# Interleaving two tensors through SBUF: eight tiles with rows of 31.5 KiB and a ninth small one, in place of eight tiles with rows of 32 KiB

## The chip, the cores and the metric

The kernel runs on one core of a Trainium2 chip. The metric is the device time of one execution in microseconds (us), the median of several runs. The profile comes from one execution that the hardware profiler recorded; its times count from the first instruction.

## What is computed

Two inputs x and y of shape 32 x 256 x 1024 in fp32 (33.5 MB each) are woven into one output of 32 x 256 x 2048: even places of the last dimension from x, odd places from y.

```python
result = np.zeros((batch, seq, dim * 2), dtype=np.float32)
result[..., 0::2] = x
result[..., 1::2] = y
```

Seen flat, each of the three tensors is one contiguous run, and element i of x and of y go to elements 2i and 2i+1 of the output. So the work can be cut at any element, without regard to the shape.

## The kernel before

The flat inputs are cut into n = 8 tiles of 128 partitions by W = 8192 columns, 4 MiB each: a partition's row is 32 KiB, contiguous in memory, and the next partition's row follows directly on it (`rows`, L18 to L20). The output tile that belongs to it has rows of 64 KiB; it is made and stored in two pieces, of 4096 input columns each, so a store moves 128 rows of 32 KiB that stand 64 KiB apart.

On chip there are two buffers each for x, y and output pieces (`xt`, `yt`, `ot`, L23 to L25), every one of 32 KiB per partition. Tile k uses `xt` and `yt` number k % 2; its piece h uses `ot` number h.

Three engines carry the order of the work, each in program order:

- SP (SyncE) issues the loads: x of tile k, then y of tile k (L42 to L50). From tile 2 on, the load of x waits until the last x copy of tile k - 2 is done, and the load of y until its last y copy is (semaphore `woven`, which every copy counts up by one, four per tile).
- VectorE (DVE) weaves (L52 to L65). For each piece it copies the columns of x into the even places of `ot[h]` (L62) and the columns of y into the odd ones (L65). Ahead of the x copy it waits for the load of x and for the store that used `ot[h]` before (`osem[h]`); ahead of the first y copy of a tile for the load of y.
- ACT (ScalarE) issues the stores (L67 to L73), each when both copies of its piece are done.

The first tile's x is loaded in two halves, one issued on SP (L38) and one on ACT (L41). ACT also issues a tiny transfer of 16 rows of 512 B straight from x into the output (L40), whose bytes the first store later overwrites. The first transfer on each of the two engines is moved ahead into the program's opening block (L91 to L110), so that it starts before the engines meet.

At the end ACT waits for the last store from `ot[0]` and clears the semaphores (L75 to L78); SP waits for the last store from `ot[1]` and counts its semaphore down (L79). SP's transfers run on the DMA queue called q1 in the profile, ACT's on q10; both feed the same 16 DMA engines.

Of the kernel before, what the change touches and what calls it, by code (L numbers as in the profile page):

```python
# [3 lines left out]


def _interleave(nc, x, y, out):
    P = 128
    W = 8192
    H = W // 2  # L10

    total = 1
    for s in x.shape:
        total *= s
    n = total // (P * W)
    assert n * P * W == total

    def rows(ap, names, k):  # L18
        flat = ap.rearrange("b s d -> (b s d)")
        return flat[k * names : (k + 1) * names].rearrange("(p w) -> p w", p=P)  # L20

    fp32 = mybir.dt.float32
    xt = [nc.alloc_sbuf_tensor(f"xt{b}", [P, W], fp32).ap() for b in (0, 1)]  # L23
    yt = [nc.alloc_sbuf_tensor(f"yt{b}", [P, W], fp32).ap() for b in (0, 1)]
    ot = [nc.alloc_sbuf_tensor(f"ot{b}", [P, W], fp32).ap() for b in (0, 1)]  # L25

    xsem = [nc.alloc_semaphore(f"xsem{b}") for b in (0, 1)]
    hsem = nc.alloc_semaphore("hsem")
    tsem = nc.alloc_semaphore("tsem")
    ysem = [nc.alloc_semaphore(f"ysem{b}") for b in (0, 1)]  # L30
    woven = nc.alloc_semaphore("woven")
    osem = [nc.alloc_semaphore(f"osem{b}") for b in (0, 1)]

    xs = [rows(x, P * W, k) for k in range(n)]
    ys = [rows(y, P * W, k) for k in range(n)]
    os_ = [rows(out, 2 * P * W, k) for k in range(n)]

    nc.sync.dma_start(out=xt[0][:, :H], in_=xs[0][:, :H]).then_inc(xsem[0], 16)  # L38
    few = (slice(0, P, P // 16), slice(0, 128))
    nc.scalar.dma_start(out=os_[0][few], in_=xs[0][few]).then_inc(tsem, 16)  # L40
    nc.scalar.dma_start(out=xt[0][:, H:], in_=xs[0][:, H:]).then_inc(hsem, 16)  # L41
    for k in range(n):  # L42
        b = k % 2
        if k >= 2:
            nc.sync.wait_ge(woven, 4 * (k - 2) + 3)
        if k:
            nc.sync.dma_start(out=xt[b], in_=xs[k]).then_inc(xsem[b], 16)
        if k >= 2:
            nc.sync.wait_ge(woven, 4 * (k - 2) + 4)
        nc.sync.dma_start(out=yt[b], in_=ys[k]).then_inc(ysem[b], 16)  # L50

    for k in range(n):  # L52
        b = k % 2
        for h in (0, 1):
            c = slice(h * H, (h + 1) * H)
            if h == 0:
                nc.vector.wait_ge(xsem[b], 16 * (k // 2 + 1))
            elif k == 0:
                nc.vector.wait_ge(hsem, 16)
            if k:  # L60
                nc.vector.wait_ge(osem[h], 16 * k)
            nc.vector.tensor_copy(out=ot[h][:, 0::2], in_=xt[b][:, c]).then_inc(woven, 1)  # L62
            if h == 0:
                nc.vector.wait_ge(ysem[b], 16 * (k // 2 + 1))
            nc.vector.tensor_copy(out=ot[h][:, 1::2], in_=yt[b][:, c]).then_inc(woven, 1)  # L65

    nc.scalar.wait_ge(tsem, 16)  # L67
    for k in range(n):
        for h in (0, 1):
            nc.scalar.wait_ge(woven, 4 * k + 2 * h + 2)  # L70
            nc.scalar.dma_start(
                out=os_[k][:, h * W : (h + 1) * W], in_=ot[h]
            ).then_inc(osem[h], 16)  # L73

    nc.scalar.wait_ge(osem[0], 16 * n)  # L75
    used = sorted(s.num for s in [*xsem, hsem, tsem, *ysem, woven, osem[0]])
    assert used == list(range(used[0], used[-1] + 1)), used
    nc.scalar.sem_clear(range(used[0], used[-1] + 1))  # L78
    nc.sync.nop(nofuse=True).wait_op(osem[1], 16 * n, "sem-ge").then_inc(  # L79
        osem[1], -16 * n  # L80
    )


def kernel(tc, x, y, out):
    nc = tc.nc
    tc.close()
    tc.compile()

    _interleave(nc, x, y, out)

    blocks = nc.main_func.blocks  # L91
    for engine in (mybir.EngineType.SP, mybir.EngineType.Activation):
        opening = blocks[0].instructions
        at, moved = next(
            (b, i)
            for b in blocks[1:]
            for i in b.instructions
            if i.engine == engine and i.opcode == "DMACopy"
        )
        assert not (moved.sync_info and moved.sync_info.on_wait)  # L100
        body = at.instructions
        body.remove(moved)
        gate = next(
            n
            for n, i in enumerate(opening)
            if i.engine == engine and i.opcode == "Drain"
        )
        opening.insert(gate, moved)
        at.instructions = body
        blocks[0].instructions = opening  # L110


# [1 line left out]
_INS = ['x', 'y']  # L114
_OUTS = [((32, 256, 2048), 'float32')]


# [23 lines left out]
```

## Time and profile before

| | us |
|---|---|
| median of 3 runs (lowest, highest) | 314.57 (314.43, 314.57) |
| span of the profiled execution | 313.0 |
| median of the runs less that span | 1.57 |
| DVE busy | 72.6 |
| idle of DVE ahead of the x copies, in all | 180.2 |
| idle of DVE ahead of the y copies, in all | 45.4 |
| one copy of 128 x 4096, x and y | 2.295 and 2.292 |
| store of 4 MiB, issue to landing, median | 29.1 |
| load of x, of y, 4 MiB, issue to landing, median | 43.7 and 60.9 |
| data moved | 134.23 MB |
| mean rate over the span | 429 GB/s |

The profiled execution has no time of its own beside its span; what a run takes around the span is seen in the third row. How to read the page: its DMA line gives the busy share of the 16 DMA engines in 40 equal slices, in tenths; the queue lines give packets, megabytes and the time of the packets as a share of 16 engines' span. The table by stage gives, for a stretch of time, the busy time of each engine with the number of instructions in brackets, the granted TensorE clock (not used here), the DMA share and the rate. A line of groups or of the order of time names the source line, the engine, the operation, the tile written and the tile read.

### The profile page before, as it was taken

What the parts mean: (1) busy time and instruction counts of PE and PEld (TensorE: products, weight loads), DVE (VectorE), ACT (ScalarE), POOL (GpSimd) and SP (SyncE); (2) the same over time, 40 slices, a digit from 0 to 9 for tenths busy, and PEclk for the clock granted to TensorE, in tenths of its full rate; (3) what the DMA queues carried; (4) which work ended last, traced back from release to release, by engine and by line L of the source; (5) the groups of instructions that cost most, each with busy time, mean ns of one, the idle gap of its engine ahead of it and who ended that gap; (6) DMA issues with size and microseconds to landing.
All of it is one profiled execution on the core that took longest, in us unless ns stands there. A gap on an engine that the chain in (4) does not pass through costs nothing.

```text
span 313.0 us, 115 instructions
## 1 busy us (share of the span) xinstructions
DVE 72.6 (23%) x32; POOL 0.2 (0%) x4
## 2 busy tenths in 40 slices
DVE  0216002231022410325003250031501305013510
POOL 0000000000000000000000000000000000000000
DMA  8999999999999999999999999999999999999998
GB/s 336 435 435 402 465 406 452 419 448 423 435 435 419 452 402 469 402 469 402 465 406 452 419 448 423 435 435 419 452 402 469 402 469 402 465 406 452 419 448 356
DMA packets 4784, 134.23 MB, mean 429 GB/s; under 512 B 544, under 2 KB 560, under 8 KB 560
## 3 DMA queue, kind: packets, MB, share of 16 engines
q10 hardware_dynamic: 2480, 69.22, 51.2%
q1 hardware_dynamic: 2304, 65.01, 48.5%
HBM read 67.12 MB, written 67.12 MB: 429 GB/s over the span
## 4 chain that ended last, share of the span: by engine, by line
DMA 82%; DVE 12%; issue 0%
DMA out_dram<-ot 76%; DVE ot L65 6%; DMA yt<-in_y_dram 6%; DVE ot L62 6%
## 5 line engine op out<-in xcount | busy, mean ns | idle before, releaser
L62 DVE COPY ot<-xt 128x4096 f32<-128x4096 f32 x16 | 36.7, 2295 | 180.2 <-DMA out_dram<-ot 171.5
L65 DVE COPY ot<-yt 128x4096 f32<-128x4096 f32 x16 | 36.7, 2292 | 45.4 <-DMA yt<-in_y_dram 45.4
L125 POOL MEMSET const-bfloat16-1.0<- 128x1 bf16 x1 | 0.1, 101 | 0.0
L125 POOL MEMSET const-uint8-127<- 128x1 uint8 x1 | 0.1, 101 | 0.0
L125 POOL MEMSET const-float32-1.0<- 128x1 f32 x1 | 0.1, 99 | 0.0
L125 POOL MEMSET const-float32-0.0<- 128x1 f32 x1 | 0.1, 98 | 0.2 <-issue 0.2
## 6 DMA issues: line engine op xcount, KB each, us to landing
out_dram<-ot ACTq DMA_DIRECT2D x16, 4096.0 KB, 29.1
yt<-in_y_dram SPq DMA_DIRECT2D x8, 4096.0 KB, 60.9
xt<-in_x_dram SPq DMA_DIRECT2D x7, 4096.0 KB, 43.7
xt<-in_x_dram SPq DMA_DIRECT2D x1, 2048.0 KB, 8.7
xt<-in_x_dram ACTq DMA_DIRECT2D x1, 2048.0 KB, 17.5
out_dram<-in_x_dram ACTq DMA_DIRECT2D x1, 8.0 KB, 6.1
```

Of the source, the lines that this page charges most:

```text
L62: nc.vector.tensor_copy(out=ot[h][:, 0::2], in_=xt[b][:, c]).then_inc(woven, 1)
L65: nc.vector.tensor_copy(out=ot[h][:, 1::2], in_=yt[b][:, c]).then_inc(woven, 1)
L125: nc = _bacc.Bacc("TRN2", target_bir_lowering=False, num_devices=1)
```

## The change

W becomes 8064, so a row is 31.5 KiB. The columns per partition in all, 65,536, are eight times 8064 and 1024 left over, which make a ninth tile (rows of 4 KiB in x and in y, of 8 KiB in the output). The first eight tiles are woven and stored in two pieces of 4032 columns, the ninth in one piece of 1024, so there are 17 pieces in place of 16. Piece i uses `ot[i % 2]`. The waits are the same ones, counted by pieces; the ninth tile's loads wait for the last copies of the seventh (number 6), like every other load for the tile two before. The last piece is now in `ot[0]`, so the two closing waits change places and the semaphores are allocated in the order that keeps the cleared ones together. The buffers shrink with W.

```diff
-    W = 8192
-    H = W // 2
+    W = 8064
...
-    n = total // (P * W)
-    assert n * P * W == total
+    assert total % P == 0
+    cols = total // P
+    widths = [W] * (cols // W)
+    if cols % W:
+        widths.append(cols % W)
+    n = len(widths)
...
+    fx, fy, fo = flat(x), flat(y), flat(out)
+    at = [P * sum(widths[:k]) for k in range(n)]
+
+    def rows(ap, k, scale=1):
+        a, w = scale * at[k], scale * widths[k]
+        return ap[a : a + P * w].rearrange("(p w) -> p w", p=P)
...
+    pieces = []
+    for k, w in enumerate(widths):
+        step = w // 2 if w > W // 2 else w
+        pieces += [(k, c, c + step) for c in range(0, w, step)]
+    last = {}
+    for i, (k, _, _) in enumerate(pieces):
+        last[k] = i
+    m = len(pieces)
+    end = (m - 1) % 2
...
     for k in range(n):
         b = k % 2
         if k >= 2:
-            nc.sync.wait_ge(woven, 4 * (k - 2) + 3)
+            nc.sync.wait_ge(woven, 2 * last[k - 2] + 1)
         if k:
-            nc.sync.dma_start(out=xt[b], in_=xs[k]).then_inc(xsem[b], 16)
+            load(xt[b], fx, k, xsem[b])
         if k >= 2:
-            nc.sync.wait_ge(woven, 4 * (k - 2) + 4)
-        nc.sync.dma_start(out=yt[b], in_=ys[k]).then_inc(ysem[b], 16)
+            nc.sync.wait_ge(woven, 2 * last[k - 2] + 2)
+        load(yt[b], fy, k, ysem[b])
...
+    for i, (k, a, e) in enumerate(pieces):
+        b = k % 2
+        if a == 0:
+            nc.vector.wait_ge(xsem[b], 16 * (k // 2 + 1))
+        elif k == 0:
+            nc.vector.wait_ge(hsem, 16)
+        if i >= 2:
+            nc.vector.wait_ge(osem[i % 2], 16 * (i // 2))
+        o = ot[i % 2][:, : 2 * (e - a)]
+        nc.vector.tensor_copy(out=o[:, 0::2], in_=xt[b][:, a:e]).then_inc(woven, 1)
+        if a == 0:
+            nc.vector.wait_ge(ysem[b], 16 * (k // 2 + 1))
+        nc.vector.tensor_copy(out=o[:, 1::2], in_=yt[b][:, a:e]).then_inc(woven, 1)
...
+    for i, (k, a, e) in enumerate(pieces):
+        nc.scalar.wait_ge(woven, 2 * i + 2)
+        nc.scalar.dma_start(
+            out=rows(fo, k, 2)[:, 2 * a : 2 * e], in_=ot[i % 2][:, : 2 * (e - a)]
+        ).then_inc(osem[i % 2], 16)
...
-    nc.scalar.wait_ge(osem[0], 16 * n)
+    nc.scalar.wait_ge(osem[1 - end], 16 * (m // 2))
...
+    turns = (m + 1) // 2
+    nc.sync.nop(nofuse=True).wait_op(osem[end], 16 * turns, "sem-ge").then_inc(
+        osem[end], -16 * turns
+    )
```

`load(tile, ap, k, sem)` issues on SP the load of the first `widths[k]` columns of a tile.

## The prediction

> **What bounds the kernel now.** I read the page first, then the busy table by stage, then the packet view of single stretches, the waits and the order of time at the end. The page:
>
> ```profile
> span 313.0 us, 115 instructions
> ...
> DMA  8999999999999999999999999999999999999998
> ...
> DMA packets 4784, 134.23 MB, mean 429 GB/s; under 512 B 544, under 2 KB 560, under 8 KB 560
> ...
> q10 hardware_dynamic: 2480, 69.22, 51.2%
> q1 hardware_dynamic: 2304, 65.01, 48.5%
> ```
>
> The 16 DMA engines are busy from end to end, and the two queues' shares add to 99.7%. The chain of waits says the same in another way: 82% of it is DMA, nearly all stores. VectorE (DVE) is busy for 72.6 of 313.0 us, and what it idles for is the stores:
>
> ```profile
> DVE ot L62 <- DMA out_dram<-ot: 171.5, 14, 19.3
> DVE ot L65 <- DMA yt<-in_y_dram: 45.4, 8, 11.0
> ```
>
> That alone doesn't yet say that the stores wait for nobody. The table by stage does (stretch, its length, DVE and POOL busy, clock, DMA share, GB/s):
>
> ```profile
> 0.00:2.00 2.00, 0.00 (x0) 0.20 (x4) 1.00 0.62 123
> 2.00:24.00 22.00, 4.27 (x2) 0.00 (x0) 1.00 1.03 441
> 24.00:30.00 6.00, 4.73 (x3) 0.00 (x0) 1.00 0.92 355
> ...
> 106.04:144.75 38.71, 9.08 (x4) 0.00 (x0) 1.00 1.00 433
> 144.75:183.49 38.74, 9.09 (x5) 0.00 (x0) 1.00 1.00 433
> ...
> 287.60:303.30 15.70, 6.79 (x3) 0.00 (x0) 1.00 1.01 434
> ```
>
> From 30 us on the share is 1.00 and the rate 433 GB/s, whether loads and stores mix (106 to 183) or stores run alone (287 to 303). So no wait of any engine reaches the end: the sum of the DMA engines' work does. Only two places run below that rate, the first 2 us and the stretch from 24 to 30, where the first store joins.
>
> **The price of a row.** The page's packets can be counted out. Each row of a transfer is one packet, and each transfer adds 16 small ones, its completion counts. Per engine: 16 half rows of the first x tile (16 KiB), 7 x 8 rows of x, 8 x 8 of y and 16 x 8 of stores at 32 KiB, one row of 512 B, 34 completions: 299, and 16 x 299 = 4784. One tile in the steady stretch is 32 rows and 4 completions per engine in 38.72 us (the mean of the two stretches above). The trace's packet records give a completion 9 ns, so a row costs (38,720 - 36) / 32 = 1,209 ns, or 37.8 ns per KiB. The records themselves show a 32 KiB row lasting 1,213 ns, a 16 KiB row 611 ns and a 512 B row 27 ns.
>
> **The change part by part.**
>
> 1. *Rows of 31.5 KiB.* The same 264 rows per engine, each 1/64 shorter: 256 whole-row equivalents lose 18.9 ns each, 4.84 us. The bytes taken off are those of the ninth tile: per engine 16 rows of 4 KiB (x and y) and 8 of 8 KiB (store) are 128 KiB, at 37.8 ns per KiB 4.84 us again. Bytes are conserved, so these two cancel, and what counts is what a row costs beside its bytes.
> 2. *24 more rows per engine.* Their fixed cost is not in the trace for these sizes, so from both sides. Below: in one stretch of 1,209 ns (7.25 to 8.46 us) the records show two 16 KiB rows per engine, as much time as one 32 KiB row: fixed cost 0. Above: the 512 B row has 27 ns, of which 18.9 are its bytes: 8 ns, so 24 x 8 = 0.20 us. Between them, 611 less half of 1,213 is 4.5 ns; the new rows lie nearer in size to that one, so 24 x 4.5 = 0.11 us.
> 3. *Three more transfers.* 3 x 9 ns of completions, 0.03 us. The issues (0.33 us each by the order of time) are on SP and ACT, which carry nothing else. On SP the ninth tile's x waits for tile 6's last x copy and its y for the copy after; behind them stand only the closing wait, so nobody is held up. On ACT the last store's wait has the wait for the other buffer and the clearing of semaphores behind it; that clearing took 64 ns at 303.4 us, and moves to about 2.4 us ahead of the end (the time of the last store's 8 rows of 8 KiB). Still hidden.
> 4. *DVE.* Its 32 long copies become 1/64 shorter (36 ns each, hidden under the DMA) and two of 1,024 columns come. A quarter of 2.29 us is 0.57 us; above, it cannot be more than the long copy. They are hidden if point 5 holds.
> 5. *The tail.* Here the change could open a hole. Before, the end looks so:
>
> ```profile
> 280.42 2.29 DVE L62 COPY ot<-xt 128x4096 f32<-128x4096 f32 x1 [14.98 <-DMA out_dram<-ot]
> 287.61 2.30 DVE L65 COPY ot<-yt 128x4096 f32<-128x4096 f32 x1 [4.90 <-DMA yt<-in_y_dram]
> 293.70 2.30 DVE L62 COPY ot<-xt 128x4096 f32<-128x4096 f32 x1 [3.80 <-DMA out_dram<-ot]
> 295.91 2.29 DVE L65 COPY ot<-yt 128x4096 f32<-128x4096 f32 x1
> ```
>
> The last load lands at 287.61 and about 21 store rows per engine (25.05 us at 1.209) remain. Afterwards x and y of the ninth tile stand behind that load, call its landing E, and share the engines with those stores. How they share decides when they land. The packet records show strict turns, one row of each queue: from 8.5 to 18 us the 16 KiB rows of the first x tile's second half go one for one with 32 KiB rows of y. That is why its 2 MiB needed so long against the same 2 MiB of the first half:
>
> ```profile
> xt<-in_x_dram SPq DMA_DIRECT2D x1, 2048.0 KB, 8.7
> xt<-in_x_dram ACTq DMA_DIRECT2D x1, 2048.0 KB, 17.5
> ```
>
> So each 4 KiB row (0.15 us) waits for a 31.5 KiB store row (1.19 us): x of the ninth tile lands at E + 8 x 1.34 = E + 10.7, y at E + 21.5. Buffer 0 comes free when the store before the last long one lands, after 5 + 8 rows, E + 17.4. The x copy fits between; the y copy ends at E + 22.1 and the last store is issued. The long stores still have 21 - 16 = 5 rows, until E + 21.5 + 5 x 1.19 = E + 27.4. So the last store has 5.3 us from issue to first row before a hole opens. The trace bounds what it needs: 1.0 us (first transfer of the program, engines idle) to 4.6 us (first store: issued at 24.41, first row at 29.05, behind rows of the other queue). It fits by both ends, by 0.7 us at the worst. Cost 0.
>
> Sum: 0.11 + 0.03 = +0.14 us on the span of 313.0. The median of the runs is 314.57, 1.6 us above that span; nothing in the change touches what lies around the span, so the forecast is 314.57 + 0.14 = **314.7 us**.
>
> The Trainium skill (DMA: Bandwidth & Descriptors, section "Queues, rings and completion order") says that an engine goes round its queues packet by packet and takes a whole packet before it switches. The one-for-one rows agree. Shared by bytes, the small loads would land within about 5 us of E and there would be no question of a hole.
>
> **Rivals.**
>
> *The ninth tile comes too late (slower).* If the turns are less even than that, say one small row for two store rows, only about 10 of the 16 small rows are through when the long stores end; then y lands after them, and the engines idle for the y copy (0.6), the issue (0.3) and the first-row latency (1.0): 1.9 us and up, to 316.6; with 4.6 us of latency 320. It decides from y landing later than E + 25.8 (latency 1.0) or E + 22.2 (latency 4.6). For it: the margin at the worst is 0.7 us, and no 4 KiB row is in the trace. Against: every mixed stretch in the records goes in strict turns. Chance 0.13.
>
> *An odd row costs as much as a full one (slower).* If an engine works in units of 1 KiB or more from the row's start, 31.5 KiB takes the 1,209 ns of 32, and the 4.84 us of point 1 are not given back: 319.5. The trace cannot exclude it, as 16 and 32 KiB are whole multiples; the 512 B row at 27 ns speaks against any unit of 1 KiB. Chance 0.09.
>
> *The pitch itself costs now (faster).* Rows stand 32 KiB apart in the inputs and 64 KiB apart in the output, and an uneven pitch could take away conflicts in memory. What there is to win is what exceeds the usual duration: summed over the records and divided by 16, 0.58 us for 32 KiB rows (nearly all at 26 to 29 us, when the first store joins) and 0.76 us for the 16 KiB rows (at the start). Both gone: 314.7 - 1.34 = 313.4; with the 0.44 us in which engines idle as well, 312.9. Against: those excesses look like first accesses, and in the steady stretch the same pitch shows no stretched row at all. Chance 0.11.
>
> [...]
>
> *The change doesn't do what it says:* were a row of 31.5 KiB cut in two packets, two halves cost no more than a whole (point 2), so the time would be the forecast's.
>
> **How the numbers follow.** Forecast 0.67, late tile 0.13, odd row 0.09, pitch 0.11. A measurement of this kernel can tell about 0.2% from no change, that is 313.94 to 315.20. So faster 0.11, within 0.67, slower 0.22. The forecast's own range is 314.5 to 315.1 (fixed cost 0 to 8 ns a row, and the runs' spread of 0.14). The range for 8 in 10 goes down to 313.9, half of what the pitch could give, and up to 316.9, which takes in the late tile at its lower latency; the odd row and the full gain of the pitch stay outside.
>
> **What would show it.** Packets: 4784 + 16 x 27 = 5216, and 592 under 512 B. Rows of 31.5 KiB lasting near 1,194 ns (right), 1,213 (odd row costs a full one). Steady stretch still at 433 GB/s with a tile in 38.1 us. The last DVE copy near 305 us, well ahead of the last long store's landing near 310.5, and a DMA share of 1.00 until then; if the share falls there, the late tile is it. If the stretch from 24 to 30 us rises from 355 GB/s, the pitch mattered. I would be wrong outright if the rate in the steady stretch moved either way.

## The result, and the profile after

The changed kernel takes 315.68 us (median of 6 runs, 315.52 to 316.94), the kernel before 314.50 (6 runs, 314.32 to 314.62): 1.0045 times as long, with a 95% interval of 1.0032 to 1.0057. That is 1.2 us slower, inside the range for 8 in 10 (313.9 to 316.9), but not the forecast's own case (314.7, within 0.2%), which had a chance of 0.67. The profiled run is the longest of the six; its span is 315.6 us, those of the others 314.2 to 314.5. The size of what follows is therefore read from the medians, and its kind from the trace.

The page:

```profile
span 315.6 us, 121 instructions
...
DMA  8999999999999999999999999999999999999996
...
DMA packets 5216, 134.23 MB, mean 425 GB/s; under 512 B 592, under 2 KB 608, under 8 KB 864
...
q10 hardware_dynamic: 2624, 69.18, 50.8%
q1 hardware_dynamic: 2592, 65.05, 48.4%
```

Packets and small packets are the forecast's 5216 and 592. The same bytes move. What differs is the last slice, 6 tenths in place of 8. The table by stage shows it closer. First the end of the kernel before, then of the changed one (stretch, length, DVE and POOL, clock, DMA share, GB/s):

```profile
309.50:312.00 2.50, 0.00 (x0) 0.00 (x0) 1.00 0.97 419
312.00:313.00 1.00, 0.00 (x0) 0.00 (x0) 1.00 0.01 0
```

```profile
309.50:312.00 2.50, 0.00 (x0) 0.00 (x0) 1.00 0.76 324
312.00:313.00 1.00, 0.00 (x0) 0.00 (x0) 1.00 0.63 262
313.00:314.00 1.00, 0.00 (x0) 0.00 (x0) 1.00 0.17 74
314.00:315.00 1.00, 0.00 (x0) 0.00 (x0) 1.00 0.08 33
```

A row counts in the stretch in which it starts, so a stretch as short as two rows can read high or low. Still, before, no row starts after 312. Afterwards the share falls in steps: 0.17 of 16 engines is some three engines, 0.08 about one. The other 13 have finished, and the kernel waits for the rest. No engine stood idle ahead of that: at every quarter of a microsecond from 304 to 312 us the packet records have 16 rows or more running at once, in both kernels.

The order of time shows where that begins. The x copy that waits for the very first store, before and after:

```profile
48.07 2.29 DVE L62 COPY ot<-xt 128x4096 f32<-128x4096 f32 x1 [19.34 <-DMA out_dram<-ot]
```

```profile
48.88 2.26 DVE L83 COPY ot<-xt 128x4032 f32<-128x4032 f32 x1 [20.15 <-DMA out_dram<-ot]
...
303.22 0.69 DVE L83 COPY ot<-xt 128x1024 f32<-128x1024 f32 x1 [6.47 <-DMA out_dram<-ot]
307.20 0.70 DVE L86 COPY ot<-yt 128x1024 f32<-128x1024 f32 x1 [3.28 <-DMA yt<-in_y_dram]
```

The first store is shorter by 1/64 and yet lands 0.8 us later. A store lands when the last of 16 engines has counted its completion, and the trace's records have all 16. Before, they lie 0.42 us apart for the first store and 0.42 for the last: the engines stay in step for the whole kernel. After, they lie 1.9 us apart for the first store and 2.8 for the last. (The records name the queue of a row, not its engine, but rows follow one another without a gap, so 16 chains can be put together; where two cross, they may be exchanged. The spread of completions doesn't depend on that.)

So between 24 and 49 us some engines fall behind, and they don't catch up. The work isn't shared out again: after 313 us some three engines still have rows while 13 stand idle. Part of the spread at the first store is only order, a load row taken ahead of a store row, and comes back when the loads are done (in the second trace of this kernel, below, it falls from 2.5 to 1.3 us); what is left at the last store is time.

### The profile page after: what moved, and what is told of

Read it like the earlier page. It is cut to its first block, busy times and chain, and to the rows that moved or that the text cites. A ratio compares the mean times of both kernels' runs of the same rounds, so it can differ in the third digit from the quotient of the medians.

```text
span 315.6 us, 121 instructions
## 1 busy us (share of the span) xinstructions
DVE 72.9 (23%) x34; POOL 0.2 (0%) x4
## 2 busy tenths in 40 slices
DMA packets 5216, 134.23 MB, mean 425 GB/s; under 512 B 592, under 2 KB 608, under 8 KB 864
## 4 chain that ended last, share of the span: by engine, by line
DMA 86%; DVE 11%; issue 0%
DMA out_dram<-ot 66%; DMA yt<-in_y_dram 20%; DVE ot L86 6%; DVE ot L83 5%
## 5 line engine op out<-in xcount | busy, mean ns | idle before, releaser
L83 DVE COPY ot<-xt 128x4032 f32<-128x4032 f32 (+1 forms) x17 | 36.9, 2169 | 187.4 <-DMA out_dram<-ot 178.4
L86 DVE COPY ot<-yt 128x4032 f32<-128x4032 f32 (+1 forms) x17 | 36.8, 2166 | 47.6 <-DMA yt<-in_y_dram 47.6
```

What stands on the lines that cost most here:

```text
L83: nc.vector.tensor_copy(out=o[:, 0::2], in_=xt[b][:, a:e]).then_inc(woven, 1)
L86: nc.vector.tensor_copy(out=o[:, 1::2], in_=yt[b][:, a:e]).then_inc(woven, 1)
```

## The experiments

Twelve runs, all built from the changed kernel's code: one has it as it is, six alter only W or the list of widths, two also the places of the rows in memory, and three add a small store or a small copy. All are compared with the kernel before on the same chip (314.5 us in each comparison). Three leave out a part of the data; their times are held against a time worked out for the data they move. From the second group on the diffs show the added lines alone, and `...` marks what is left out.

**First: is it the ninth tile, the pitch or the length of the rows?**

```diff
-    W = 8064
+    W = 8192
...
-    widths = [W] * (cols // W)
-    if cols % W:
-        widths.append(cols % W)
+    widths = [W] * 7 + [W - 1024, 1024]
```

> Seven tiles with rows of 32 KiB as before, an eighth with rows of 28 KiB, and the same ninth tile of 1024 columns at the end. Theory A (the uneven pitch puts the 16 DMA engines out of step, and the slowest one ends the kernel): the completions of one transfer stay within 0.5 us of each other for the first seven tiles, and the time is that of before plus the 0.14 us of the extra rows, 314.6 (314.4 to 314.9). Theory B (the ninth tile at the end, its small rows and late y, is what costs): about 1.2 us over before, 315.7, as in the changed kernel.

Measured: 314.56, ratio 1.0003 (0.9994 to 1.0011), completions 0.50 us apart from first store to last. The ninth tile is there with its late y copy and its 24 small rows per engine, and costs 0.06 us (-0.2 to +0.35). Theory B is out. Its y copy starts where the turns of rows had put it (305):

```profile
301.90 0.70 DVE L81 COPY ot<-xt 128x1024 f32<-128x1024 f32 x1 [5.84 <-DMA out_dram<-ot]
305.48 0.69 DVE L84 COPY ot<-yt 128x1024 f32<-128x1024 f32 x1 [2.89 <-DMA yt<-in_y_dram]
```

```diff
-    if cols % W:
-        widths.append(cols % W)
```

> The changed kernel without its ninth tile: the last 1024 columns of each partition are neither loaded nor stored, 128 KiB per DMA engine less. In step that is 314.5 - 4.84 = 309.7. Theory A (engines out of step from the pitch): 1 us above that, 310.7 (310.3 to 311.5), with completions of one transfer 2 to 3 us apart. Theory B (the ninth tile costs): 309.7 (309.4 to 310.0).

Measured: 310.29 (310.10 to 310.48), 0.6 us above 309.66. Completions are 2.06 us apart for the first store, and 0.83 for the last. Theory B is out here too. Theory A holds in kind; the time is just below the range it gave.

```diff
-    if cols % W:
-        widths.append(cols % W)
...
-    at = [P * sum(widths[:k]) for k in range(n)]
+    Q = 8192
+    at = [P * Q * k for k in range(n)]
...
-        return ap[a : a + P * w].rearrange("(p w) -> p w", p=P)
+        whole = ap[a : a + P * scale * Q].rearrange("(p w) -> p w", p=P)
+        return whole[:, :w]
```

> The same 31.5 KiB rows and no ninth tile, but the rows stand 32 KiB apart in the inputs and 64 KiB apart in the output, as before; the last 128 columns of each row are left out. Theory A in the form that the pitch in memory is the cause: engines in step, 309.7 (309.4 to 310.0), completions within 0.5 us. In the form that the length of the row is the cause: as without the ninth tile at the pitch of 31.5 KiB, 310.7. Theory B: 309.7 too, but then the kernel without the ninth tile is there as well.

Measured: 310.37 (310.32 to 310.50), spread 2.43 us at the first store. The pitch is that of before, and the loss is there.

```diff
-    W = 8064
+    W = 8192
...
-    widths = [W] * (cols // W)
-    if cols % W:
-        widths.append(cols % W)
+    widths = [W] * 7
...
-    at = [P * sum(widths[:k]) for k in range(n)]
+    Q = 8320
+    at = [P * Q * k for k in range(n)]
...
-        return ap[a : a + P * w].rearrange("(p w) -> p w", p=P)
+        whole = ap[a : a + P * scale * Q].rearrange("(p w) -> p w", p=P)
+        return whole[:, :w]
```

> Rows of 32 KiB as before, but 32.5 KiB apart in the inputs and 65 KiB in the output, seven tiles in place of eight (the eighth tile and the columns between the rows are left out). In step it would be 314.5 - 38.72 = 275.8. Theory A, pitch: 276.6 to 277.2 and completions 2 to 3 us apart. Theory A, length of the row: 275.8 and completions within 0.5 us. Theory B: 275.8.

Measured: 275.85 (275.58 to 275.98) against the 275.8 worked out, spread 0.61 us throughout. So nothing of the loss, and no gain, is seen to come from the pitch in memory. So far the loss goes with the rows' length.

**Second: which rows, and when?**

The changed kernel with no edit:

> The changed kernel once more, for a second trace of its engines. All theories: 315.5 to 315.9. Theory A as the runs so far leave it (rows of 31.5 KiB, not their pitch, put the engines out of step): completions of one transfer 2 us or more apart from the first store on, though on other engines and by other amounts than in the first trace if the step is lost by chance at the first store.

Measured: 315.52 (314.84 to 315.82), ratio 1.0029 (1.0020 to 1.0039). Spread 2.5 us at the first store (the records don't tell on which engines). The end now has one step fewer than in the first trace:

```profile
309.50:312.00 2.50, 0.00 (x0) 0.00 (x0) 1.00 0.83 353
312.00:313.00 1.00, 0.00 (x0) 0.00 (x0) 1.00 0.55 229
313.00:314.00 1.00, 0.00 (x0) 0.00 (x0) 1.00 0.08 33
314.00:315.00 1.00, 0.00 (x0) 0.00 (x0) 1.00 0.00 0
```

The runs of one kernel differ by 1 us, where the 31 of before in the same comparison differ by 0.5, and the best of them, 314.84, comes near the forecast. How many engines fall behind, and how far, changes from run to run.

```diff
+    W = 8192
...
+    widths = [W] * 2 + [8064] * 6 + [768]
```

> Two tiles with rows of 32 KiB, then six with rows of 31.5 KiB and a ninth of 768 columns. Theory C (the engines lose step at the first store, 24 to 30 us, because row ends of 31.5 KiB rows fall just where the first store's rows come up, and some engines take one more load row first; the length of later rows doesn't matter): in step as before, completions within 0.7 us, 314.6 (314.4 to 314.9). Theory L (rows of 31.5 KiB lose step wherever they run): 315.2 to 315.8 and spreads that begin after the second tile.

Measured: 314.60, ratio 1.0003 (0.9994 to 1.0011), spread 0.46 us at the first store and at the last. Six tiles of 31.5 KiB rows run in step. Theory L is out: the length of the rows does nothing later.

```diff
+    W = 8192
...
+    widths = [8064] * 2 + [W] * 6 + [256]
```

> The reverse: two tiles with rows of 31.5 KiB, then six with rows of 32 KiB and a ninth of 256 columns. Theory C: out of step from the first store on, completions of a store about 2 us apart, 315.2 to 315.8. Theory L: 314.5 to 314.8, in step at least from the third tile on.

Measured: 315.17 (314.88 to 316.05), ratio 1.0024 (1.0014 to 1.0033), spread 2.47 us at the first store, 1.2 at the last. The time lies just below the 315.2 that theory C gave as its least. What the first two tiles lose, six tiles of 32 KiB rows don't mend.

```diff
+    W = 8192
...
+    nc.scalar.wait_ge(xsem[0], 16)
+    nc.scalar.wait_ge(tsem, 16)
+    nc.scalar.dma_start(out=rows(fo, 0, 2)[few], in_=xt[0][few]).then_inc(tsem, 16)
...
+        if k == 2:
+            nc.sync.wait_ge(tsem, 32)
...
+    nc.scalar.wait_ge(tsem, 32)
```

> Rows of 32 KiB throughout (seven tiles of 8192 columns would be eight: this is the changed code with W = 8192, so eight tiles, no ninth), and a tiny store of 16 rows of 512 B from the x buffer into the output at about 9 us, overwritten by the first store. If the load rows that last 0.4 to 0.7 us too long at 26 to 29 us pay for the first transfer out of the chip's own memory, whatever its size, they move to about 9 us and shrink there or stay: 314.0 to 314.5. If they pay for the first full store beside loads, nothing moves: 314.5.

Measured: 314.62, ratio 1.0003 (0.9994 to 1.0012). The tiny store was issued at 8.52 us, but its rows ran at 19.8 to 20.3 us, behind the load rows of its own queue; that is still 9 us ahead of the first full store's rows. Nothing moved: no row of 32 KiB lasts over 20 ns too long before 24 us, and at 26 to 28 us they last too long by 0.79 us an engine in the mean, against 0.55 to 0.81 in the other five traces that stay in step. So the long load rows go with the first full store beside loads, not with the first store of any size. As an improvement it fails.

**Third: what at the first store?** By the chains, in the kernels that stay in step every engine spends some 0.4 to 1.0 us more than usual on its last load rows ahead of its first store row, and that store row comes 4.6 to 5.4 us after the issue. In the others some engines take one load row more ahead of their first store row, which comes 5.6 to 7 us after the issue, and in six of those eight traces such engines spend 1.4 to 1.7 us there (in the first of the changed kernel and in one below the chains cross too often to say). This can be counted in the packet view of 28.3 to 30.5 us. (The end of that window lies 5.5 to 6.5 us after the issue, so the count can miss an engine that is only a little late: in the changed kernel's first trace one first store row lies beyond it, and five more come 5.6 to 5.7 us after the issue.) Of the kernel before:

```profile
q10 hardware_dynamic: 16, 0.52, 56.0%
q1 hardware_dynamic: 11, 0.36, 37.9%
```

and of the one without the ninth tile:

```profile
q1 hardware_dynamic: 16, 0.52, 56.3%
q10 hardware_dynamic: 12, 0.39, 41.4%
```

q10 carries the stores: before, all 16 engines have begun their first store row by then; here 12 have. In that trace the four late ones spend about 1.5 us where the other twelve spend 0.5 to about 1, and four engines end at 308.3 to 308.4 us where the others end at 307.6 to 307.9. That is about the 0.6 us.

```diff
+    W = 8192
...
+    widths = [8064] + [W] * 7 + [128]
```

> Only the first tile has rows of 31.5 KiB (so the first two stores have them, and x and y of that tile); seven tiles of 32 KiB rows and a ninth of 128 columns follow. The load rows that pass while the first store comes up (x of the second tile) are of 32 KiB. Theory S (the length of the store's rows decides): some engines take an extra load row ahead of their first store row, as 1 to 4 of 16 did in each kernel that begins with 31.5 KiB, 315.0 to 315.8. Theory R (the load rows that pass at that time decide): all 16 first store rows within 4.6 to 5.4 us of the issue, 314.6 (314.4 to 314.8).

Measured: 315.10 (314.65 to 315.84), ratio 1.0021 (1.0012 to 1.0030). One tile with short rows is enough, and the load rows that pass at that time are of 32 KiB.

```diff
+    W = 8192
...
+    widths = [W, 8064] + [W] * 6 + [128]
```

> Only the second tile has rows of 31.5 KiB: the first store's rows are of 32 KiB, and the load rows that pass while it comes up are of 31.5. Theory R: some engines a row late, 315.0 to 315.8. Theory S: all 16 in step, 314.6 (314.4 to 314.8). Theory C (where the row ends fall against the store's coming, by chance) gives no clear answer for this one and the one before.

Measured: 314.59, ratio 1.0001 (0.9992 to 1.0011), spread 0.33 us. Theory R is out. S (the first store's rows, or those of the loads that feed it) and C (the moment) are left.

```diff
+    scrap = nc.alloc_sbuf_tensor("scrap", [P, 1024], fp32).ap()
...
+        if i == 0:
+            nc.vector.tensor_copy(out=scrap, in_=xt[b][:, 0:1024])
```

> The changed kernel with one more copy of 1024 columns (0.5 to 0.7 us, into a tensor that nothing reads) ahead of the first y copy, which puts the first store about half a row later against the load rows; nothing else moves, as the loads fill that time. Theory C (row ends fall just where the store comes up): another half row of distance restores the step, 314.6 (314.4 to 314.9). Theories S and R (length of the rows): as the changed kernel, 315.2 to 315.8.

Measured: 314.95 (314.86 to 315.63), ratio 1.0016 (1.0007 to 1.0026). The median falls by 0.6 against the same kernel without the extra copy (315.52, in another comparison) and lands between the two theories. Seven of ten runs lie below the 315.2 that S and R gave as their least, six of them within 0.1 us of the 314.9 that C gave as its most, but only three inside C's range; the profiled one (315.48) has one engine late. So what theory C forecast for this kernel didn't come about: the loss became smaller and didn't go.

The same extra copy with W = 8192:

> Rows of 32 KiB in eight tiles as before, with the same extra copy ahead of the first y copy. Theory C: the first store now comes up elsewhere against the row ends and some engines should take an extra load row, 315.0 to 315.8. Theories S and R: in step as before, 314.5 (314.3 to 314.7).

Measured: 314.80 (314.45 to 315.11), ratio 1.0008 (0.9998 to 1.0018), which is too little to tell a difference by the interval, though nine of its ten runs lie above 314.6 us and only six of the 31 of the kernel before. The trace tells it. In the profiled run (315.08) all rows but the small test rows are 32 KiB or halves of it, and the packet view has

```profile
q10 hardware_dynamic: 14, 0.46, 48.9%
q1 hardware_dynamic: 9, 0.29, 31.4%
```

Two engines of 16 miss the turn, and the first store's completions lie 2.1 us apart; in the six traces that stay in step none of 96 does. So the short row isn't needed for engines to fall out of step: in this trace a first store issued 0.5 us later (24.93 against 24.41) is enough. That is what theory C says, and S as the whole cause is out. Whether a short row adds to it at the same moment, no run shows.

All fourteen traces together, the times being medians of their runs (the first store row counts if it starts between 28.3 and 30.5 us):

| kernel | first store rows begun | completions of the first store, us apart | time over its in-step time, us |
|---|---|---|---|
| before | 16 | 0.42 | 0 |
| 32 KiB rows and a ninth tile | 16 | 0.50 | 0.06 |
| 32 KiB rows at 32.5 KiB | 16 | 0.61 | 0.05 |
| first two tiles of 32 KiB | 16 | 0.46 | 0.1 |
| early tiny store | 16 | 0.45 | 0.1 |
| only the second tile of 31.5 KiB | 16 | 0.33 | 0.1 |
| changed, first trace | 15 | 1.9 | 1.2 |
| changed, again | 13 | 2.5 | 1.0 |
| without the ninth tile | 12 | 2.1 | 0.6 |
| the same at a pitch of 32 KiB | 15 | 2.4 | 0.7 |
| first two tiles of 31.5 KiB | 13 | 2.5 | 0.7 |
| only the first tile of 31.5 KiB | 14 | 2.3 | 0.6 |
| changed, first store later | 15 | 1.8 | 0.4 |
| before, first store later | 14 | 2.1 | 0.3 |

(In-step time: 314.5, less 4.84 for the two without their last columns; 275.8 for seven tiles.) Two groups, and nothing between them: 16 and at most 0.61 us, or fewer and at least 1.8. None of the nine that do the whole work has a lower median than the kernel before.

One thing sorts all fourteen after the fact. In the six traces that stay in step the first store is issued at 24.30 to 24.46 us; in the eight others at 23.97 to 24.17 (five of them) or at 24.49 to 25.01 (three). That fits the moment as the cause, but the six share a first tile of 32 KiB rows, the upper gap is only 0.03 us wide, and no run was made to test it. Nor may the kernel before be proof against the loss: one of its 31 runs in the last comparison took 315.63 us, and no trace shows what happened there.

What stays open. Why an engine misses the turn at one moment and not at another: where its row ends stand against the store's issue does not separate late engines from others in these traces, so theory C says that the moment matters, not which moment is safe. Nor is it settled why the changed kernel loses 1.0 to 1.2 us where its parts lose 0.6 to 0.7. In its first trace, load rows are stretched later as well: after 35 us 33 of them last over 20 ns too long, 4.7 us in all, and the spread of the completions grows from 1.9 to 2.8 us. In its second trace there are 2 such rows, 0.3 us in all, and the spread doesn't grow. These would add where they fall on an engine that is already late, but no run takes them by themselves.

## Why the prediction was right in its range and wrong in its likeliest case

- *"So no wait of any engine reaches the end: the sum of the DMA engines' work does."* This is the step that failed. It took 16 engines for one. Each has its own 264 rows (288 after the change), nothing is shared out again, as the end of the changed kernel shows, and the kernel ends with the slowest. Before, the two readings give the same number, since the engines stay within 0.42 us; nothing on the page tells them apart, and a DMA share of 1.00 holds in both. The completions of one transfer tell them apart.
- *The stretch from 24 to 30 us* was named as one of two places below full rate, and counted in the forecast as the same before and after. It was looked at only as something to win (the pitch), not to lose. It is where the loss arises. The sign set for the pitch (a rise from 355 GB/s) came, and meant nothing: rows count where they start, the changed kernel is slower, and the kernel with short rows at the old pitch has 387 there. The changed kernel's line:

```profile
24.00:30.00 6.00, 4.74 (x3) 0.00 (x0) 1.00 1.01 376
```

- *Rows of 31.5 KiB, conserved bytes*: right. They last 1,194 ns as forecast, the steady stretch runs at 432 to 434 GB/s, and six tiles of them cost nothing. The odd row (319.5) is out.
- *24 more rows and three completions, +0.14 us*: not contradicted; the ninth tile with 32 KiB rows measured +0.06 (-0.2 to +0.35).
- *The tail*: right. The strict turns put the last y copy near 305, and it starts at 305.48 in the in-step kernel with a ninth tile and at 305.33 in the changed kernel's second trace. In its first trace it starts at 307.20, as the completions wait for the late engines, and still all 16 engines have rows until 312. The late tile is out as the cause: its place in the sum was 0, and 0 it was. The Trainium skill (DMA: Bandwidth & Descriptors, section "Queues, rings and completion order") has engines change queues after each packet. That agrees: in the second trace, while stores were queued, the 4 KiB rows took their turns one for one with rows eight times as long, one in 1.34 us.
- *The pitch (313.4)*: out. At 32.5 KiB the time (275.85) is the one worked out for 32 KiB (275.8) within 0.2 us. The Trainium skill (DMA: Bandwidth & Descriptors, section "Latency and other measured facts") gives rates for row pitches from 512 KiB to 8 MiB, with a loss of about half at 4 MiB; no run here has such a pitch, and at 32 KiB nothing of the kind shows.
- The slower side had 0.22, for two mechanisms that both proved absent. A result 1.2 us slower came by a third, which the prediction doesn't have. So it is luck that the range held it: its upper end, 316.9, was set by the late tile.

## What to carry to other kernels

Where the DMA engines bound a kernel, its end is that of the slowest of 16, so read the spread of one transfer's completions beside the DMA share. Here the last store's were 0.3 to 0.6 us apart in the traces that stayed in step, where the engines can be taken for one, and 0.8 to 2.8 us in the others, where one engine's delay is the kernel's. An engine that loses time once, at a change such as the first store beside running loads, keeps it to the end; so anything that moves that moment, even 0.5 us of it or a row shorter by 1/64, can cost some tenths of a per cent that no count of bytes shows. The versions here that altered only later tiles, and left that moment alone, were free of it (314.56 to 314.60 us).

## What the runs showed that was not expected

- Where the first full store comes up beside running loads, load rows last too long by 0.55 to 0.99 us an engine in the mean, in all fourteen traces; a tiny store whose rows ran 9 us earlier doesn't take it away.
- With 4 KiB rows in one queue and 31.5 KiB rows in the other, one engine's completion of a 512 KiB load came 15.7 us after the first engine's, in the changed kernel's first trace, since an engine with stores still queued takes a long row between any two small ones, and the others, whose stores had run out for a moment, ran their small rows in a stretch.
- One extra copy of 0.69 us on DVE, wholly hidden under DMA, moved the median by -0.6 us in one kernel and by +0.3 us in the other; the second by itself is within the noise.
